# RMSNorm and matmul on one core: six of each sixteen tiles turned on VectorE in place of four

## The chip, the cores and the metric

The kernel runs on one core of one Trainium2 chip. The metric is device time in microseconds for one execution. Within a core, TensorE multiplies matrices, VectorE, ScalarE and GpSimd work element by element, and DMA engines move data between the chip's memory and the core; SyncE issues the DMA here.

## The reference

```python
# x: (16, 1024, 512) float32, weight: (512, 768) float32, gamma: (512,)
def reference(x, gamma, weight, eps):
    rms = np.sqrt(np.mean(x ** 2, axis=-1, keepdims=True) + eps)
    x_norm = x / rms * gamma
    return np.matmul(x_norm, weight).astype(np.float32)
```

There are 16,384 rows of 512 features. A tile is 128 rows, so there are 128 tiles. Gamma is multiplied into the weights once; the division by rms is done on the product, since it is one factor per row.

## The kernel before

Rows arrive in groups of sixteen tiles (`XG`) in two buffers. GpSimd casts a stretch to bf16. The matmul needs the features on the partitions, so each tile has to be turned. Two bf16 features are moved together as one 32-bit word, so a tile has two blocks of 128 by 128 words.

Most tiles are turned on TensorE: each word block is transposed into PSUM, between two matmuls of an earlier pair of tiles, and VectorE evicts the pair to SBUF. From the second group on, the last four tiles of each sixteen are turned on VectorE instead: GpSimd casts them to a buffer of their own, and VectorE moves them in sixteen steps, each of which transposes 32 by 32 blocks of all four tiles:

```python
    def quad_of(j):
        return j // 2 if (2 * j) % XG >= XG - 4 and 2 * j >= XG else None

    def cast_quad(q):
        quads[q] = quad_in.tile([P, 4, D], BF16, name="xq")
        nc.gpsimd.tensor_copy(out=quads[q], in_=held(x_tiles, XG, 4 * q, 4))
        turned = quad_out.tile([P, 4, 2, P, 2], BF16, name="xTq")
        # ... words and out_words: the same tiles seen as 32-bit words
        for tokens in range(0, P, B):            # B = 32
            for features in range(0, P, B):
                quad_moves.append((out_words[features:features + B, :, tokens:tokens + B],
                                   words[tokens:tokens + B, :, features:features + B]))

    def move_quad(n):
        for _ in range(min(n, len(quad_moves))):
            dst, src = quad_moves.pop(0)
            nc.vector.transpose(out=dst, in_=src)

    def matmul(i, k, acc, lo, hi):
        nc.tensor.matmul(out=acc[:, lo:hi], lhsT=xT_tiles[i // 2][:, i % 2, k // 2, :, k % 2],
                         rhs=w_bf[:, k, lo:hi], start=(k == 0), stop=(k == K - 1))
```

A tile takes eight matmuls (four feature blocks by 512 and 256 columns) into one of three accumulators in PSUM. ScalarE scales the even tiles by 1/rms and VectorE the odd ones, and the result is stored in stretches of eight tiles, shorter ones at the start and the end. The order of work is fixed by the program, engine by engine. The loop runs over pairs of tiles:

```python
        for j in range(1, NP):                                  # NP = 64 pairs
            load_until((2 * j + AHEAD + XG - 1) // XG * XG)     # AHEAD = 20
            if j in (1, 2):
                cast(4 * j + 4, nc.gpsimd, 4)
            elif j % 8 == 4 and j + 4 < NP:
                cast(2 * j + 8, nc.gpsimd, 8)
            elif j % 8 == 6 and j + 2 < NP:
                cast(2 * j + 12, nc.gpsimd, 4)
            if (2 * j + 2) % XG == 0 and 2 * j + 2 < NT:
                cast_quad((2 * j + 2 + XG - 4) // 4)
            elif 2 * j >= XG:
                move_quad(3)
            # ... squares of pair j + 4 on ScalarE, and every fourth pair root and reciprocal
            # ... pairs 1 to 3 left out here
            elif j + 2 < NP and quad_of(j + 2) is None:
                feed = feeder([j + 2], two)       # transposes and eviction of pair j + 2
            else:
                feed = None
            for i, engine in ((2 * j, nc.scalar), (2 * j + 1, nc.vector)):
                a = accumulator()
                matmuls(i, a, range(K), feed)
                finish_tile(i, a, engine)         # scaling, and the store behind a stretch
```

Of the kernel before, what the change touches and what calls it, by code (L numbers as in the profile page):

```python
# [12 lines left out]
F32 = mybir.dt.float32  # L13
BF16 = mybir.dt.bfloat16
# [4 lines left out]
def kernel(  # L19
# [8 lines left out]
    nc = tc.nc  # L28
    P = 128

    x = x.flatten_outer_dims()
    out = out.flatten_outer_dims()
    N, D = x.shape
    _, O = out.shape
    K = D // P
    NT = N // P
    NP = NT // 2
    XG, OG = 16, 8
# [30 lines left out]
    quad_in = ctx.enter_context(tc.tile_pool(name="quad_in", bufs=2))  # L69
    quad_out = ctx.enter_context(tc.tile_pool(name="quad_out", bufs=2))  # L70
# [4 lines left out]
    x_tiles, xb_tiles, tp_tiles, rstd_of, xT_tiles, o_tiles, norm_sums = {}, {}, {}, {}, {}, {}, {}  # L75

    def held(tiles, group, i, n=1):
        return tiles[i // group][:, i % group:i % group + n, :]
# [8 lines left out]
    def load_until(i):  # L87
        while starts and starts[0] < i:
            load(starts.pop(0))

    def cast(i, engine, n=1):
        if i // 8 not in xb_tiles:
            xb_tiles[i // 8] = xbp.tile([P, 8, D], BF16, name="xb")
        engine.tensor_copy(out=xb_tiles[i // 8][:, i % 8:i % 8 + n, :], in_=held(x_tiles, XG, i, n))  # L94
# [13 lines left out]
    def norms(i, n):  # L108
        ssq = stats.tile([P, 10], F32, name="ssq")
        for t in range(n):  # L110
            square(i + t, ssq[:, t:t + 1])
        root(i, n, ssq)
# [32 lines left out]
    def transpose_tile(i):  # L145
        for h in range(2):
            transpose_word(i // 2, i % 2, h)
        evac(i // 2, i % 2, 1)

    B = 32
    quads, quad_moves = {}, []

    def quad_of(j):
        return j // 2 if (2 * j) % XG >= XG - 4 and 2 * j >= XG else None

    def cast_quad(q):
        quads[q] = quad_in.tile([P, 4, D], BF16, name="xq")
        nc.gpsimd.tensor_copy(out=quads[q], in_=held(x_tiles, XG, 4 * q, 4))  # L160
        turned = quad_out.tile([P, 4, 2, P, 2], BF16, name="xTq")
        for n in range(2):
            xT_tiles[2 * q + n] = turned[:, 2 * n:2 * n + 2]
        words = quads.pop(q).rearrange("p t d -> p (t d)").bitcast(F32).rearrange("p (a w) -> p a w", w=P)
        out_words = turned.rearrange("p t h m c -> p (t h m c)").bitcast(F32).rearrange("p (a m) -> p a m", m=P)
        for tokens in range(0, P, B):
            for features in range(0, P, B):
# [8 lines that stand above are left out]
    def scale(engine, dst, src, r):  # L176
        if engine is nc.scalar:
            nc.scalar.mul(out=dst, in_=src, mul=r)  # L178
        else:
            nc.vector.tensor_single_scalar(out=dst, in_=src, scalar=r, op=mybir.AluOpType.mult)  # L180
# [3 lines left out]
    def accumulator():  # L184
        return opsum.tile([P, 2, WIDE], F32, name=f"ops{next(turns) % 3}").rearrange("p a b -> p (a b)")
# [16 lines left out]
    def matmuls(i, acc, ks, feed=None):  # L202
        for k in ks:
            matmul(i, k, acc, 0, WIDE)
            if feed:
                feed()
            matmul(i, k, acc, WIDE, O)

    def finish_tile(i, acc, engine):
        scale(engine, out_tile(i), acc[:, :O], rstd_of[i])  # L210
        store(i)


    def feeder(pairs, gaps, alone=False):
        queue = [(j, t, h) for j in pairs for t in range(2) for h in range(2)]
        calls = iter(gaps)

        def feed():
            for _ in range(next(calls)):
                j, t, h = queue.pop(0)  # L220
                transpose_word(j, t, h)
                if alone and h == 1:
                    evac(j, t, 1)
                elif (t, h) == (1, 1):
                    evac(j)
        return feed

    with tc.manual_schedule():
        g_row = singles.tile([2, P, 2], F32)
        nc.scalar.dma_start(out=g_row, in_=gamma.rearrange("(h w c) -> h w c", w=P, c=2))  # L230
        nc.scalar.preload_act_table(AF.Sqrt)  # L231
        wv = weight.rearrange("(h w c) o -> w h (c o)", w=P, c=2)
        w_f32 = singles.tile([P, K, O], F32)

        def load_weights(h):
            nc.sync.dma_start(out=w_f32[:, 2 * h:2 * h + 2, :].rearrange("p c o -> p (c o)"), in_=wv[:, h, :])  # L236

        load_until(2)
        load_weights(0)
        load_weights(1)  # L240
        load_until(2 * XG)


        warm = singles.tile([P, WIDE], BF16)
        nc.vector.memset(warm, 0.0)
        eps_sb = singles.tile([P, 1], F32)
        nc.vector.memset(eps_sb, float(eps))  # L247
        ident_f = singles.tile([P, P], F32)
        make_identity(nc, ident_f)
        spare = accumulator()  # L250

        def warm_up(n):
            for _ in range(n):
                nc.tensor.matmul(out=spare[:, :WIDE], lhsT=warm[:, :P], rhs=warm, start=True, stop=True)  # L254

        w_bf = singles.tile([P, K, O], BF16)

        def weights(k, engine, lo=0, hi=O):
            scale(engine, w_bf[:, k, lo:hi], w_f32[:, k, lo:hi], g_sb[:, k % 2, k // 2:k // 2 + 1])


        warm_up(6)
        gp = tpsum.tile([P, 2, 2], F32, name="tp")
        for c in range(2):
            nc.tensor.transpose(out=gp[:, c, :], in_=g_row[:, :, c], identity=ident_f[:2, :2])  # L265
        g_sb = singles.tile([P, 2, 2], F32)
        nc.vector.tensor_copy(out=g_sb, in_=gp)  # L267
        cast(0, nc.gpsimd)
        cast(1, nc.gpsimd)
        cast(2, nc.gpsimd, 2)  # L270
        norms(0, 2)
        warm_up(4)
        transpose_tile(0)
        transpose_tile(1)
        warm_up(2)
        weights(0, nc.vector, 0, WIDE)
        weights(0, nc.vector, WIDE, O)
        weights(1, nc.scalar)
        acc = [accumulator() for _ in range(2)]
        for i in range(2):  # L280
            matmuls(i, acc[i], [0, 1])
        weights(2, nc.vector)
        weights(3, nc.scalar)
        norms(2, 2)
        cast(4, nc.gpsimd, 2)
        matmuls(0, acc[0], [2, 3])
        finish_tile(0, acc[0], nc.scalar)
        matmuls(1, acc[1], [2, 3], feeder([1], [2, 2], alone=True))
        finish_tile(1, acc[1], nc.vector)
        cast(6, nc.gpsimd, 2)  # L290

        mid, one, two, both = ([0, 0, 1, 1, 0, 1, 1, 0], [1, 1, 0, 1, 1, 0, 0, 0], [1, 0, 1, 0, 1, 0, 1, 0],
                               [1, 1, 1, 1, 1, 1, 1, 1])
        for j in range(1, NP):
            load_until((2 * j + AHEAD + XG - 1) // XG * XG)
            if j in (1, 2):
                cast(4 * j + 4, nc.gpsimd, 4)
            elif j % 8 == 4 and j + 4 < NP:
                cast(2 * j + 8, nc.gpsimd, 8)
            elif j % 8 == 6 and j + 2 < NP:  # L300
                cast(2 * j + 12, nc.gpsimd, 4)
            if (2 * j + 2) % XG == 0 and 2 * j + 2 < NT:
                cast_quad((2 * j + 2 + XG - 4) // 4)
            elif 2 * j >= XG:
                move_quad(3)
            if j < 4:
                norms(2 * j + 2, 2)
            for pair in norm_turns.get(j, []):
                norms_of_group(pair)
            if j < 3:  # L310
                feed = feeder([j + 1], mid if j == 1 else one, alone=j == 1)
            elif j == 3:
                feed = feeder([4, 5], both)
            elif j + 2 < NP and quad_of(j + 2) is None:
                feed = feeder([j + 2], two)
            else:
                feed = None
# [3 lines that stand above are left out]
                finish_tile(i, a, engine)  # L321
# [35 lines left out]
```

## Time and profile before

| | before |
|---|---|
| time, median of 3 | 210.8 us (210.73 to 211.62) |
| span of the profiled execution | 208.1 us |
| granted TensorE clock, mean | 0.991 |
| VectorE busy | 149.6 us |
| ScalarE busy | 144.5 us |
| GpSimd busy | 59.9 us |
| read and written in the chip's memory | 35.13 MB and 50.33 MB |

The page of the profile gives busy time for each engine (PE is TensorE, PEld its weight loads, DVE is VectorE, ACT is ScalarE, POOL is GpSimd), then the span in 40 slices whose digits are busy tenths, then the chain of work that ended last, and then groups of instructions: line, engine, operation, output and input, shape, count, busy time, mean in ns, and idle time ahead of them. A line of a timeline has its start in us, its length in us, engine, line of the program and operation; in square brackets stands the idle time before it and what ended that. Matmuls overlap in TensorE's pipeline, so the length of one is more than what it adds. Lengths of GpSimd are rough.

### The profile page before, as it was taken

How to read it: one execution, taken by the hardware profiler on the slowest of the kernel's cores; microseconds unless marked ns; L12 is line 12 of the kernel's file. 1: busy time of each engine (PE TensorE's matmuls, PEld its weight loads, DVE VectorE, ACT ScalarE, POOL GpSimd, SP SyncE). 2: the span in 40 equal slices, each digit the busy share in tenths (PEclk: the TensorE clock that was granted, in tenths of full speed). 3: DMA queues.
4: the chain of work that ended last, by engine and by line, in shares of the span. 5: the costliest groups of instructions: out<-in, count | busy, mean ns of one | idle time of the engine just before them, and what ended most of it. 6: DMA issues, size and time to landing. Idle time of an engine off the chain costs nothing.

```text
span 208.1 us, 3335 instructions
## 1 busy us (share of the span) xinstructions
PE 195.1 (94%) x1238; PEld 129.9 (62%) x1238; DVE 149.6 (72%) x255; ACT 144.5 (69%) x343; POOL 59.9 (29%) x34
## 2 busy tenths in 40 slices
PE   7899999996999999999999999999999999999930
PEld 2466776663666666676667666776667666776610
DVE  0456647997379984999579984999579984999520
ACT  4698897753977877677867877677867877673310
POOL 3237652003900390065200670007500373000000
PEclk9999999999999999999999999999999999999996
DMA  6999999999999999999999999999999999994996
GB/s 252 419 438 441 331 396 435 459 449 390 437 439 438 405 439 409 408 403 431 428 411 436 441 430 430 420 431 439 430 438 408 424 444 435 424 439 203 453 413 267
DMA packets 5490, 85.65 MB, mean 412 GB/s; under 512 B 610, under 2 KB 612, under 8 KB 1380
## 3 DMA queue, kind: packets, MB, share of 16 engines
q1 hardware_dynamic: 5472, 85.46, 97.4%
q8 instruction: 9, 0.15, 0.3%
q14 instruction: 5, 0.04, 0.0%
q10 hardware_dynamic: 4, 0.00, 0.0%
HBM read 35.13 MB, written 50.33 MB: 411 GB/s over the span
## 4 chain that ended last, share of the span: by engine, by line
PE 71%; DMA 21%; SPq 2%; ACT 1%; POOL 1%; DVE 0%; issue 0%; ACTq 0%; POOLq 0%
PE ops L198 63%; DMA xt<-in_x_dram 21%; PE tp L135 8%; SPq L83 1%; POOL xb L94 1%; DVE ot L180 0%; ACT jk L98 0%; SPq L236 0%; ACT ot L178 0%; POOLq L94 0%; ACTq L178 0%; ACTq L98 0%
## 5 line engine op out<-in xcount | busy, mean ns | idle before, releaser
L198 PE MATMUL ops<-w_bf,xT 128*128 128x512 bf16 (+1 forms) x800 | 147.7, 326 | 2.6 <-ACT ot L178 2.0
L198 PEld LDWEIGHTS <-xT 128*128 128x128 bf16 x800 | 78.3, 98 | 48.4 <-issue 3.0
L178 ACT ACTIVATE ot<-ops,rstd 128x768 f32<-128x768 f32 x64 | 57.6, 899 | 45.3 <-PE ops L198 44.6
L98 ACT ACTIVATE jk<-xt 128x512 bf16<-128x512 f32 x128 | 78.8, 619 | 6.2 <-DMA xt<-in_x_dram 6.2
L94 POOL CAST xb<-xt 128x2048 bf16<-128x2048 f32 (+3 forms) x21 | 46.3, 2218 | 113.0 <-DMA xt<-in_x_dram 113.0
L180 DVE TENSOR_SCALAR ot<-ops,rstd 128x768 f32<-128x768 f32 x64 | 64.8, 1013 | 12.5 <-PE ops L198 12.0
L135 PE MATMUL tp<-ident_f,xb 128*128 128x128 f32 x200 | 54.2, 276 | 0.8 <-POOL xb L94 0.7
L142 DVE COPY xT<-tp 128x1024 bf16<-128x1024 bf16 (+1 forms) x53 | 34.5, 654 | 24.8 <-PE tp L135 24.1
L174 DVE STREAM_TRANSPOSE xTq<-xq 32x256 f32<-32x256 f32 x112 | 48.7, 435 | 1.9
L198 PE MATMUL ops<-w_bf,xTq 128*128 128x512 bf16 x224 | 42.8, 326 | 0.0
L135 PEld LDWEIGHTS tp<-ident_f,xb 128*128 128x128 f32 x200 | 28.5, 143 | 4.9 <-POOL xb L94 2.5
L198 PEld LDWEIGHTS <-xTq 128*128 128x128 bf16 x224 | 22.0, 98 | 12.3
L98 ACT ACTIVATION_READ_ACCUMULATOR jk<-xt 128x1 f32 x128 | 24.4, 191 | 0.0
L160 POOL CAST xq<-xt 128x2048 bf16<-128x2048 f32 x7 | 13.3, 1894 | 0.0
L104 DVE RECIPROCAL rstd<-rms 128x8 f32<-128x8 f32 (+3 forms) x20 | 3.9, 193 | 7.7 <-ACT rms L102 7.5
L102 ACT ACTIVATE rms<-ssq,eps_sb 128x8 f32<-128x8 f32 (+3 forms) x20 | 6.0, 299 | 0.6
L254 PE MATMUL ops<-warm 128*128 128x512 bf16 x12 | 5.2, 587 | 1.2 <-DVE eps_sb L247 1.2
L254 PEld LDWEIGHTS <-warm 128*128 128x128 bf16 x12 | 1.4, 128 | 2.9 <-issue 1.7
L178 ACT ACTIVATE w_bf<-w_f,g_sb 128x768 bf16<-128x768 f32 x2 | 1.9, 935 | 1.4 <-DMA w_f<-in_weight_dram 1.1
L267 DVE COPY g_sb<-tp 128x4 f32<-128x4 f32 x1 | 0.2, 161 | 3.2 <-PE tp L265 3.2
L231 ACT ACT_TABLE_LOAD x1 | 1.3, 1283 | 1.3 <-PEq L338 1.3
L180 DVE TENSOR_SCALAR w_bf<-w_f,g_sb 128x512 bf16<-128x512 f32 (+2 forms) x3 | 1.4, 481 | 0.1
(10 smaller groups left out, 1.9 us busy)
## 6 DMA issues: line engine op xcount, KB each, us to landing
out_dram<-ot SPq DMA_DIRECT2D x13, 3072.0 KB, 15.8
xt<-in_x_dram SPq DMA_DIRECT2D x11, 2048.0 KB, 18.5
xt<-in_x_dram SPq DMA_DIRECT2D x2, 4096.0 KB, 20.2
out_dram<-ot SPq DMA_DIRECT2D x5, 1536.0 KB, 9.9
w_f<-in_weight_dram SPq DMA_DIRECT2D x2, 768.0 KB, 5.6
out_dram<-ot SPq DMA_DIRECT2D x2, 768.0 KB, 16.5
xt<-in_x_dram SPq DMA_DIRECT2D x2, 512.0 KB, 5.3
xt<-in_x_dram SPq DMA_DIRECT2D x1, 1024.0 KB, 9.2
```

The source lines that it names most:

```text
L94: engine.tensor_copy(out=xb_tiles[i // 8][:, i % 8:i % 8 + n, :], in_=held(x_tiles, XG, i, n))
L98: nc.scalar.activation(out=jk, in_=held(x_tiles, XG, i)[:, 0, :], func=AF.Square, accum_out=ssq)
L102: nc.scalar.activation(out=rms[:, :n], in_=ssq[:, :n], func=AF.Sqrt, scale=1.0 / D, bias=eps_sb)
L104: nc.vector.reciprocal(out=rstd[:, :n], in_=rms[:, :n])
L135: nc.tensor.transpose(out=tp_tiles[j][:, t, h, :], in_=words[:, lo:lo + P], identity=ident_f)
L142: nc.vector.tensor_copy(out=dst[:, t:t + n, :], in_=src[:, t:t + n, :])
L160: nc.gpsimd.tensor_copy(out=quads[q], in_=held(x_tiles, XG, 4 * q, 4))
L174: nc.vector.transpose(out=dst, in_=src)
L178: nc.scalar.mul(out=dst, in_=src, mul=r)
L180: nc.vector.tensor_single_scalar(out=dst, in_=src, scalar=r, op=mybir.AluOpType.mult)
L198: nc.tensor.matmul(out=acc[:, lo:hi], lhsT=xT_tiles[i // 2][:, i % 2, k // 2, :, k % 2], rhs=w_bf[:, k, lo:hi], start=(k == 0), stop=(k == ...
L254: nc.tensor.matmul(out=spare[:, :WIDE], lhsT=warm[:, :P], rhs=warm, start=True, stop=True)
```

## The change

Six of each sixteen tiles, three pairs in place of two, are turned on VectorE. This is meant to take more transposes from TensorE. The six are cast as one piece, one pair earlier than the four were, and the blocks that VectorE moves span six tiles instead of four, so there are still sixteen of them in a group. The two tiles between the first eight and these six are cast after them. Tiles 32 to 39 are cast as four and four instead of eight at once.

```diff
-    def quad_of(j):
-        return j // 2 if (2 * j) % XG >= XG - 4 and 2 * j >= XG else None
-
-    def cast_quad(q):
-        quads[q] = quad_in.tile([P, 4, D], BF16, name="xq")
-        nc.gpsimd.tensor_copy(out=quads[q], in_=held(x_tiles, XG, 4 * q, 4))
-        turned = quad_out.tile([P, 4, 2, P, 2], BF16, name="xTq")
-        for n in range(2):
-            xT_tiles[2 * q + n] = turned[:, 2 * n:2 * n + 2]
+    B, TURNED = 32, 6
+
+    def turned_on_vector(j):
+        return (2 * j) % XG >= XG - TURNED and 2 * j >= XG
+
+    def cast_to_turn(group):
+        first = (group + 1) * XG - TURNED
+        straight = quad_in.tile([P, TURNED, D], BF16, name="xq")
+        nc.gpsimd.tensor_copy(out=straight, in_=held(x_tiles, XG, first, TURNED))
+        turned = quad_out.tile([P, TURNED, 2, P, 2], BF16, name="xTq")
+        for n in range(TURNED // 2):
+            xT_tiles[first // 2 + n] = turned[:, 2 * n:2 * n + 2]
 ... (words, out_words and the sixteen moves as before, over six tiles)
             if j in (1, 2):
                 cast(4 * j + 4, nc.gpsimd, 4)
+            elif j == 12:
+                for i in (32, 36):
+                    cast(i, nc.gpsimd, 4)
             elif j % 8 == 4 and j + 4 < NP:
                 cast(2 * j + 8, nc.gpsimd, 8)
             elif j % 8 == 6 and j + 2 < NP:
-                cast(2 * j + 12, nc.gpsimd, 4)
-            if (2 * j + 2) % XG == 0 and 2 * j + 2 < NT:
-                cast_quad((2 * j + 2 + XG - 4) // 4)
-            elif 2 * j >= XG:
+                cast_to_turn(j // 8 + 1)
+                cast(2 * j + 12, nc.gpsimd, 2)
+            else:
                 move_quad(3)
 ...
-            elif j + 2 < NP and quad_of(j + 2) is None:
+            elif j + 2 < NP and not turned_on_vector(j + 2):
                 feed = feeder([j + 2], two)
```

More of the change, by code (lines that the diff above doesn't have):

```diff
@@ L148, in transpose_tile @@
         evac(i // 2, i % 2, 1)
-    B = 32
-    quads, quad_moves = {}, []
-    def quad_of(j):
-        return j // 2 if (2 * j) % XG >= XG - 4 and 2 * j >= XG else None
-    def cast_quad(q):
-        quads[q] = quad_in.tile([P, 4, D], BF16, name="xq")
-        nc.gpsimd.tensor_copy(out=quads[q], in_=held(x_tiles, XG, 4 * q, 4))
-        turned = quad_out.tile([P, 4, 2, P, 2], BF16, name="xTq")
-        for n in range(2):
-            xT_tiles[2 * q + n] = turned[:, 2 * n:2 * n + 2]
-        words = quads.pop(q).rearrange("p t d -> p (t d)").bitcast(F32).rearrange("p (a w) -> p a w", w=P)
+    B, TURNED = 32, 6
+    quad_moves = []
+    def turned_on_vector(j):
[7 more added lines that the diff above has]
+            xT_tiles[first // 2 + n] = turned[:, 2 * n:2 * n + 2]
+        words = straight.rearrange("p t d -> p (t d)").bitcast(F32).rearrange("p (a w) -> p a w", w=P)
         out_words = turned.rearrange("p t h m c -> p (t h m c)").bitcast(F32).rearrange("p (a m) -> p a m", m=P)
```

## The prediction

> **What bounds the kernel now.** I read the page first (busy time, the 40 slices, the chain), then the waits, then the timeline of single engines around one group of sixteen tiles. A pair j below is tiles 2j and 2j+1, and a group is eight pairs.
>
> ```profile
> PE 195.1 (94%) x1238; PEld 129.9 (62%) x1238; DVE 149.6 (72%) x255; ACT 144.5 (69%) x343; POOL 59.9 (29%) x34
> DVE  0456647997379984999579984999579984999520
> DMA  6999999999999999999999999999999999994996
> PE 71%; DMA 21%; SPq 2%; ACT 1%; POOL 1%; DVE 0%; issue 0%; ACTq 0%; POOLq 0%
> L135 PE MATMUL tp<-ident_f,xb 128*128 128x128 f32 x200 | 54.2, 276 | 0.8 <-POOL xb L94 0.7
> L174 DVE STREAM_TRANSPOSE xTq<-xq 32x256 f32<-32x256 f32 x112 | 48.7, 435 | 1.9
> ```
>
> TensorE is the bound: its longest idle stretch after the start is one of 2.01 us at 50.4 us, where ScalarE stood behind the third group of x; from 52.4 to 199.7 us it has none. DMA engines are nearly as full, and VectorE, 72% on average, has three or four slices in a row at 9 in every group. The chain shows TensorE's own rhythm:
>
> ```profile
> 71.71 5.85 PE ops L198 x36
> 77.56 0.11 PE tp L135
> 77.67 0.65 PE ops L198 x4
> ...
> 95.13 5.85 PE ops L198 x36
> ```
>
> Four matmuls take 0.65 us, a transposed word 0.11 us on top. A pair with its four words of transposing takes 8 x 0.65 / 2 + 4 x 0.11 = 3.04 us, one without them 2.60; six of the first and two of the second are 23.4 us, which is the distance of the two long stretches (95.13 - 71.71 = 23.42). The mean of 276 ns per transpose is therefore no price: matmuls overlap, and 0.11 us is what a word costs.
>
> VectorE in the stretch that turns tiles, from its timeline:
>
> ```profile
> 89.09 0.69 DVE L142 COPY xT<-tp 128x1024 bf16<-128x1024 bf16 x1
> 89.82 1.02 DVE L180 TENSOR_SCALAR ot<-ops,rstd 128x768 f32<-128x768 f32 x1
> 90.86 1.33 DVE L174 STREAM_TRANSPOSE xTq<-xq 32x256 f32<-32x256 f32 x3
> ...
> 97.09 1.34 DVE L174 STREAM_TRANSPOSE xTq<-xq 32x256 f32<-32x256 f32 x3
> 98.44 1.02 DVE L180 TENSOR_SCALAR ot<-ops,rstd 128x768 f32<-128x768 f32 x1
> 99.47 0.44 DVE L174 STREAM_TRANSPOSE xTq<-xq 32x256 f32<-32x256 f32 x1
> 100.80 1.02 DVE L180 TENSOR_SCALAR ot<-ops,rstd 128x768 f32<-128x768 f32 x1 [0.89 <-PE ops L198]
> ```
>
> Start to start, an eviction costs 0.73 us, a scaling 1.04, three blocks 1.37: 3.14 us per pair against TensorE's 3.04. VectorE is full here and slips about 0.1 us per pair. The single block at 99.47 is the sixteenth. It runs in pair 29, and the first turned pair is 30, whose first matmul starts at 100.60: 0.7 us to spare.
>
> [...] at 50.2 us ScalarE's ready scaling stood behind two squares that waited 4.32 us for DMA. [...] in the 2.01 us stall nothing passed the blocked matmul. [...] No transpose of another size is in the trace, but the evictions have a slope that fits: 420 ns at 512 bf16, 684 at 1024, which is 264 ns for 256 words of 32 bits, 1.03 ns per word.
>
> **The change, part by part.**
>
> *Transposes removed.* In each of groups 1 to 7 one pair more (13, 21, ... 61) is turned on VectorE: 4 words x 0.11 = 0.43 us less on TensorE per group. In group 1 it is lost, because TensorE then stalls at 50 us for x whose load is issued at 29.96, before anything has changed. Six remain: **-2.6 us**. Seven evictions leave VectorE.
>
> *Blocks grow.* 112 blocks go from 256 to 384 words. My estimate is 435 + 128 x 1.03 = 567 ns each; three take 1.37 + 0.40 = 1.77 us.
>
> *Blocks move.* This is the step I hold decisive. Before, moving was under its own `if`, so every pair from 8 on, except the one that casts, called move_quad(3): pairs 8 to 12 ran fifteen and pair 13 the last. Now it is the `else` of the chain of casts. In a group, pairs 7, 8, 9, 10, 11 run three each; pair 12 takes a cast branch (12 by name, later ones by j % 8 == 4) and moves nothing. The sixteenth block runs at pair 13, 21, 29, ... which is the first turned pair itself. It is emitted after the scaling of tile 2j-1, and VectorE is in order. A turned tile's first weights take all 128 partitions and all 128 tokens, so they need all sixteen blocks. TensorE has to stand from the end of pair 12 until VectorE has scaled tile 25 and moved one block.
>
> The length of that stand: the scaling of a tile starts about 0.20 us after the next tile's first matmul could have issued (tile 60's matmul at 100.60, tile 59's scaling at 100.80), 1.03 us to the next VectorE start, 0.57 for the block, and 0.18 as an estimate for the signal and the exposed weight load (weights to matmul is 0.11 at 194.2): 1.98 us.
>
> *VectorE slips first.* A pair with all its work now costs VectorE 1.77 + 0.73 + 1.04 = 3.54 us against 3.04. Set zero at the end of the last tile of pair 6, where its scaling starts on time. Scalings of the odd tiles then start at 3.54, 7.08, 10.62 and (a reciprocal falls in pair 10, whose eviction is shorter after it: 0.68 in place of 0.73) 14.11, for tiles 15 to 21. Pair 11 has no eviction: moves end at 16.92, tile 23 is scaled by 17.96. There are three accumulators, so tile 24 needs tile 21's scaling, which ends at 15.15; TensorE would start tile 24 at 14.6. That is a stall of 0.6 us. Tile 25 then ends at 17.96, its scaling at 19.0, the block at 19.57, and tile 26 starts at 19.74 where it would have started at 17.2: **2.54 us per group**, the 1.98 included.
>
> *By group.* Group 1: 19.74 us after 31.49 is 51.2, so tile 26 issues until 52.5; tile 27 waits until 52.4 for ScalarE anyway. Loss 0.1 to 0.2. Groups 2 to 6: nothing of this lies beside another wait, since TensorE had none: 5 x 2.54 = **+12.7 us**. Group 7: no cast falls in pair 60, so the last block runs there, but behind the late scaling of tile 119. TensorE loses 0.6 + 0.85 us. The store behind tile 119 is late too, about 1.9 us, and from that store on DMA carries the end (6.3 MB between 192 and 206 us): **+1.9 us**.
>
> *Casts.* Six tiles cast ahead of two make pairs 12, 20, ... ready later: 1.89 + 0.85 = 2.75 us for six (slope of 1893 and 3600 ns) plus 1.04, instead of 1.89, after landing. They are read about 10 us later. The block cast must be ready one pair earlier, at 32.5 us in group 1; it ends at 28.55 + 2.75 = 31.3. Splitting the cast of tiles 32 to 39 removes a wait of 0.26 us in a stretch that already stood. I count none.
>
> *DMA.* Bytes and order are unchanged. First halves of the loads land 24.3 to 25.3 us apart (casts at 90.43, 115.74, 140.01, 164.82), slower than TensorE's 23.4, so loads were losing their lead. A TensorE at 23.0 + 2.5 = 25.5 us per group is slower than this, and loads stop being a threat.
>
> Sum: 0.2 + 12.7 + 1.9 - 2.6 = +12.2 us; I take +11.7, as a block a little shorter takes the slip away sixteenfold.
>
> **Rivals.** (a) What the change is for: the last block is hidden, TensorE saves 2.6 us and the end moves to about 208.2. It needs the sixteenth block a pair early; the branches say otherwise. (b) DMA covers all: near 211. A DMA share of 1.00 to 1.01 from 60 to 120 us speaks for it; against it, TensorE waits for no data after 52.4, and a loss on TensorE isn't hidden by full queues. (c) Only the stand of 1.98 us, no slip before it: 5 x 1.98 - 2.6 = +7.3, 218 us. That is so if the larger blocks cost 30 to 40 ns less than estimated. (d) Blocks scale with size, 650 ns: VectorE is 16 x 0.08 = 1.3 us later in each group, and the time is near 229 us.
>
> **Range and chances.** The centre is 210.8 + 11.7 = 222.5 us. (c) gives the lower edge, 218; a little over half of the way to (d) the upper, 226.5. All but (a) and (b) are over 2% slower, so 0.95 for slower, 0.04 within 2%, 0.01 faster.
>
> **What would show it.** Right: the waits get a new row of TensorE or its weight load on VectorE's xTq line, six times, about 2 us each, at pairs 13 to 53 and none as long at 61; blocks at about 567 ns; scalings of odd tiles starting up to 2 us late in pair 11; the distance of groups near 25.5 us. Wrong: blocks done before the pair begins, waits of TensorE on ScalarE or DMA in their place, or a block far from 567 ns.

## The result and the profile after

The changed kernel takes **219.95 us** (median of 6 runs, 219.76 to 220.54) against 210.75 us for the kernel before; the ratio is 1.0439, with a 95% interval of 1.0415 to 1.0463. It is slower by 9.2 us, within the range that the prediction gave and 2.6 us under its centre.

From the page of the changed kernel, the same rows as shown of before: TensorE, the slices of VectorE and DMA, the chain by engine, and the two groups that the change touches.

```profile
PE 194.5 (89%) x1210; PEld 125.6 (58%) x1210; DVE 159.6 (73%) x248; ACT 144.6 (66%) x343; POOL 60.0 (28%) x35
DVE  0474669994799929995699947998399956999330
DMA  6999999999999999999999999999999999680996
DVE 46%; PE 26%; DMA 15%; issue 4%; ACT 3%; SPq 1%; POOL 1%; DVEq 0%; ACTq 0%
L175 DVE STREAM_TRANSPOSE xTq<-xq 32x384 f32<-32x384 f32 x112 | 63.7, 569 | 1.9
L135 PE MATMUL tp<-ident_f,xb 128*128 128x128 f32 x172 | 46.7, 277 | 0.5 <-POOL xb L94 0.5
```

TensorE has 28 transposes less and a lower share. VectorE has 10 us more to do: 15.0 us more in blocks, which take 569 ns instead of 435, and 5.1 us less in evictions. It has taken TensorE's place on the chain. DMA, which had one slice at 4 before, now has slices at 6, 8 and 0 near the end.

The list of waits of the changed kernel shows what is new (who waited for whom: us in total, times, longest):

```profile
PEld L199 <- DVE xTq L175: 13.6, 7, 2.1
PE ops L199 <- DVE xTq L175: 10.9, 7, 1.7
PE ops L199 <- DVE ot L181: 1.5, 7, 0.2
```

None of the three stood in the list of before. The first two are one event seen by the weight load and by the matmul: seven times TensorE stands for a block. The third is an accumulator that VectorE frees late. Here is one group (pairs 28 to 30), TensorE first, then VectorE:

```profile
96.82 2.76 PE L199 MATMUL ops<-w_bf,xT 128*128 128x512 bf16 x16 [0.22 <-DVE ot L181]
101.28 2.99 PE L199 MATMUL ops<-w_bf,xTq 128*128 128x512 bf16 x17 [1.70 <-DVE xTq L175]
```

```profile
95.76 1.01 DVE L181 TENSOR_SCALAR ot<-ops,rstd 128x768 f32<-128x768 f32 x1
96.80 1.74 DVE L175 STREAM_TRANSPOSE xTq<-xq 32x384 f32<-32x384 f32 x3
98.57 2.07 DVE L181 TENSOR_SCALAR ot<-ops,rstd 128x768 f32<-128x768 f32 x2
100.65 0.57 DVE L175 STREAM_TRANSPOSE xTq<-xq 32x384 f32<-32x384 f32 x1
```

Pair 28 starts at 96.82, 0.22 us after the last matmul before it had ended, when VectorE's scaling that began at 95.76 is done. Pair 28 ends at 99.58. VectorE then scales its odd tile, and only behind this, at 100.65, moves the sixteenth block. Pair 29 starts at 101.28. In time lost, each idle stretch costs 0.165 us more than it shows, because a matmul that nothing holds started about that much before the recorded end of the one ahead (in the profile of before, pair 30's first at 100.60 us, the one ahead ending at 98.65 + 2.11 = 100.76): 0.385 and 1.87 us, 2.25 in a group. The next such restart is at 126.52, so a group takes 25.24 us; TensorE's work alone takes 23.0.

### The profile page after: what moved, and what is told of

It is laid out like the page before. It is cut to its first block, busy times and chain, and to the rows that moved or that the text cites. A ratio compares the mean times of both kernels' runs of the same rounds, so it can differ in the third digit from the quotient of the medians.

```text
span 217.6 us, 3270 instructions
## 1 busy us (share of the span) xinstructions
PE 194.5 (89%) x1210; PEld 125.6 (58%) x1210; DVE 159.6 (73%) x248; ACT 144.6 (66%) x343; POOL 60.0 (28%) x35
## 4 chain that ended last, share of the span: by engine, by line
DVE 46%; PE 26%; DMA 15%; issue 4%; ACT 3%; SPq 1%; POOL 1%; DVEq 0%; ACTq 0%
PE ops L199 24%; DVE xTq L175 21%; DVE ot L181 17%; DMA xt<-in_x_dram 15%; DVE xT L142 7%; ACT jk L98 2%; PE tp L135 2%; POOL xb L94 1%; ACT ot L179 1%; SPq L83 1%; DVE rstd L104 1%; SPq L237 0%; DVEq L181 0%; SPq L196 0%; ACTq L179 0%
## 5 line engine op out<-in xcount | busy, mean ns | idle before, releaser
L199 PE MATMUL ops<-w_bf,xT 128*128 128x512 bf16 (+1 forms) x688 | 127.4, 326 | 2.0 <-DVE ot L181 1.5
L199 PEld LDWEIGHTS <-xT 128*128 128x128 bf16 x688 | 67.3, 98 | 42.8 <-issue 3.6
L199 PE MATMUL ops<-w_bf,xTq 128*128 128x512 bf16 x336 | 61.2, 326 | 11.0 <-DVE xTq L175 10.9
L94 POOL CAST xb<-xt 128x1024 bf16<-128x1024 f32 (+3 forms) x22 | 40.6, 1855 | 103.7 <-DMA xt<-in_x_dram 103.7
L175 DVE STREAM_TRANSPOSE xTq<-xq 32x384 f32<-32x384 f32 x112 | 63.7, 569 | 1.9
L199 PEld LDWEIGHTS <-xTq 128*128 128x128 bf16 x336 | 32.3, 98 | 32.6 <-DVE xTq L175 13.6
L135 PE MATMUL tp<-ident_f,xb 128*128 128x128 f32 x172 | 46.7, 277 | 0.5 <-POOL xb L94 0.5
L142 DVE COPY xT<-tp 128x1024 bf16<-128x1024 bf16 (+1 forms) x46 | 29.4, 641 | 13.5 <-PE tp L135 13.0
L135 PEld LDWEIGHTS tp<-ident_f,xb 128*128 128x128 f32 x172 | 24.6, 144 | 4.1 <-POOL xb L94 2.0
L161 POOL CAST xq<-xt 128x3072 bf16<-128x3072 f32 x7 | 19.2, 2747 | 12.5 <-DMA xt<-in_x_dram 12.5
## 6 DMA issues: line engine op xcount, KB each, us to landing
out_dram<-ot SPq DMA_DIRECT2D x5, 1536.0 KB, 10.2
```

Source lines behind the costliest of these rows:

```text
L135: nc.tensor.transpose(out=tp_tiles[j][:, t, h, :], in_=words[:, lo:lo + P], identity=ident_f)
L142: nc.vector.tensor_copy(out=dst[:, t:t + n, :], in_=src[:, t:t + n, :])
L161: nc.gpsimd.tensor_copy(out=straight, in_=held(x_tiles, XG, first, TURNED))
```

## The experiments

All times are medians. The kernel before, measured beside each of them on the same chip, took 210.6 to 210.9 us, and each ratio is to that, with its 95% interval.

**1. The sixteenth block one pair earlier.** Moving gets its own condition again:

```diff
             elif j % 8 == 6 and j + 2 < NP:
                 cast_to_turn(j // 8 + 1)
                 cast(2 * j + 12, nc.gpsimd, 2)
-            else:
+            if j % 8 != 6:
                 move_quad(3)
```

> The changed kernel with moving under its own condition (every pair except those with j % 8 == 6), so that the sixteenth block runs in pair 12, 20, ... as it does in the last group of the changed kernel. Theory (the place of the block in VectorE's order makes TensorE stand): the stand of about 2 us behind one scaling goes; what stays is what the changed kernel shows in its last group, 0.21 us for an accumulator and about 0.7 to 1.0 us at the first turned pair, because VectorE is late. A group then takes 23.0 + 1.2 = 24.2 us on TensorE, and the time is near 215.3 us (214 to 216.5). Rival (VectorE simply has too much to do in a group, wherever the block stands): within 1 us of the changed kernel's 220. Rival (DMA sets the new pace): also near 220, with TensorE or ScalarE waiting for x.

Measured: 214.91 us (ratio 1.017, 1.013 to 1.021). The waits of this run and TensorE in the same group:

```profile
PE ops L199 <- DVE xTq L175: 4.7, 7, 0.7
PE ops L199 <- DVE ot L181: 1.6, 7, 0.2
```

```profile
95.89 2.76 PE L199 MATMUL ops<-w_bf,xT 128*128 128x512 bf16 x15 [0.22 <-DVE ot L181]
99.32 2.99 PE L199 MATMUL ops<-w_bf,xTq 128*128 128x512 bf16 x17 [0.67 <-DVE xTq L175]
```

The stand of 1.70 us became 0.67, a group takes 24.21 us, and 5.0 of the 9.2 us are back. What is left has another cause: the block now runs ahead of the scaling of the tile before it (98.69 against 99.29 us), and VectorE is simply not done yet. Runs 4 and 5 test this.

**2. The old kernel with its last block late.** Nothing is larger and nothing is saved; the leftover block alone moves into the first turned pair:

```diff
-            elif 2 * j >= XG:
+            elif 2 * j >= XG and j % 8 != 5:
                 move_quad(3)
```

> The kernel before, four tiles turned and small blocks, with its one leftover block put off from pair 13, 21, ... to pair 14, 22, ..., the first turned one. Nothing else differs: same instructions, same bytes. Theory: TensorE stands in all seven groups for 0.20 + 1.03 + 0.44 + 0.18 = 1.85 us, 13 us together, of which about 1 is hidden at the tail: 222 to 224 us. Rival (larger blocks and VectorE's load make the loss, not the place of the block): within 1 us of 210.8.

Measured: 220.94 us (ratio 1.0469, 1.043 to 1.0508), 10.2 us more and 1 us under the range expected. TensorE in this run:

```profile
105.23 0.39 PE L198 MATMUL ops<-w_bf,xTq 128*128 128x512 bf16 x1 [1.56 <-DVE xTq L174]
```

The place of a single block of 0.44 us costs as much as the whole change. The distance of these restarts, 80.07 to 105.23 us, is 25.16, so each costs 25.16 - 23.42 = 1.74 us and not 1.85: a weight load of 0.1 us that I had counted isn't exposed (the block ends at 104.73 + 0.44 = 105.17, the matmul starts at 105.23). VectorE kept program order there: the block stood behind a scaling for which VectorE waited 1.34 us, though the three blocks of the same tiles ahead of it had run at 99.99 us (scaling at 103.70, block at 104.73). In the first group the restart came at 54.91 where before it was 53.67, 1.24 us later, as TensorE had resumed 0.49 us earlier from its stall at 50 us. At the end 1.4 us are hidden: from VectorE's last scaling to the end of the span it is 7.0 us here (211.31 of 218.3) and 8.4 before.

**3. The split cast alone.** The kernel before with tiles 32 to 39 cast as four and four:

```diff
+            elif j == 12:
+                for i in (32, 36):
+                    cast(i, nc.gpsimd, 4)
             elif j % 8 == 4 and j + 4 < NP:
                 cast(2 * j + 8, nc.gpsimd, 8)
```

> The kernel before with only the cast of tiles 32 to 39 split in four and four. Expected by every theory: within 0.4 us of 210.8; the wait of 0.26 us of TensorE's weight load for GpSimd at 53.9 us goes. If it were worth more, the cast would have held up the third group.

Measured: 210.17 us (ratio 0.996, 0.9938 to 0.9983). It is a gain of half a microsecond, a little more than expected. In its profile TensorE resumes at 51.86 us instead of 52.37, but the x that it waited for also landed 0.5 us earlier in that run, before the cast in question began. TensorE's last matmul ends 0.60 us earlier than before (199.04 against 199.64), 0.51 of it there at the restart already, and the span is 208.0 against 208.1. So the profile leaves 0.1 us for the cast, and where the half microsecond of the medians comes from stays open.

**4 and 5. Taking work off VectorE.** As run 1, and one odd tile per group, then two, is scaled on ScalarE. Run 5 takes the pairs with j % 8 of 0 and 2, which are the first and third pair counted from 8, not the "second and sixth" of its text:

```diff
-            for i, engine in ((2 * j, nc.scalar), (2 * j + 1, nc.vector)):
+            for i, engine in ((2 * j, nc.scalar),                                 # run 4
+                              (2 * j + 1, nc.scalar if j > 8 and j % 8 == 2 else nc.vector)):
+            for i, engine in ((2 * j, nc.scalar),                                 # run 5
+                              (2 * j + 1, nc.scalar if j >= 8 and j % 8 in (0, 2) else nc.vector)):
```

> As the run with the block one pair ahead, and in each group from the second on the odd tile of the third pair (21, 37, ...) is scaled on ScalarE instead of VectorE. That takes 1.04 us from VectorE ahead of the sixteenth block. Theory: VectorE is no longer late, TensorE stands at most 0.1 us per group, a group takes 23.0 to 23.2 us, and the transposes saved show as 2 to 2.6 us: 208 to 209.5 us. Rival (DMA, whose first halves landed every 24.3 to 25.3 us before, then sets the pace): TensorE and ScalarE wait for x in the late groups and the time stays at 210 to 212. Rival (VectorE overloaded): 214 or more.

Measured: 210.78 us (ratio 0.9991, 0.9976 to 1.0006). The stands shrank, but a group takes 23.29 us, 0.1 more than expected and 0.3 above the 22.99 that TensorE's work needs, and the time did not fall under that of before. In the profile, another part of this is TensorE's clock. Windows of run 4 around its stall (length; busy time of TensorE, weight loads, VectorE, ScalarE and GpSimd; then granted clock, DMA share, GB/s):

```profile
50.00:52.00 2.00, 0.12 (x2) 0.00 (x0) 0.00 (x0) 2.00 (x5) 1.94 (x2) 1.00 1.11 473
52.00:54.00 2.00, 1.84 (x10) 1.11 (x10) 0.29 (x1) 2.00 (x6) 2.00 (x2) 0.86 1.00 430
54.00:56.00 2.00, 2.00 (x9) 1.15 (x8) 0.93 (x2) 1.65 (x6) 2.00 (x1) 0.50 1.03 442
```

Behind an idle stretch of 2.04 us the granted clock fell to 0.50 for 3.4 us. At 0.50 four matmuls and a transpose took 1.50 us (transposes at 53.89 and 55.39 us), at 1.00 they took 0.76 (56.87 and 57.63), so about half of the 3.4 us, some 1.7, is my estimate of the matmul time that it costs. TensorE ends at 200.22 us, 0.6 later than before.

> As the run with one scaling on ScalarE, but two odd tiles per group go there, those of the second and the sixth pair after the moving starts being counted from pair 8: j % 8 is 0 and 2 (tiles 17, 21, 33, 37, ...). In the run before this one TensorE still stood about 0.28 us per group for the sixteenth block, and in its profile the granted clock fell to 0.50 for some 3.5 us behind the idle stretch at 50 us. Theory: with 1.04 us more off VectorE the stand is gone, a group takes 23.0 us on TensorE in place of 23.29, and the time is 207.5 to 209.3 us (the clock's dip adds about 1 us when it comes). Rival (DMA sets the end once TensorE is faster): no stand of TensorE for VectorE, but ScalarE and TensorE wait for x in the last groups, and 210 to 211 us. Rival (ScalarE is overloaded, 2 x 0.90 us more per group): TensorE waits for ScalarE's scaling, 211 or more.

Measured: 210.79 us (ratio 0.998, 0.9952 to 1.0009). Here TensorE no longer waits for a block at all: the turned pairs begin at 73.69, 96.67, 119.66 us, 22.99 apart, which is the pace that the change was meant to give. TensorE ends 3 us earlier than before, at 196.64 instead of 199.64, and the time stands. The rival with DMA had this time right, but not its sign, as TensorE waits for no x behind 52.01 us. Windows of the kernel before at its end:

```profile
188.00:192.00 4.00, 4.00 (x27) 2.49 (x25) 3.85 (x8) 1.56 (x2) 0.00 (x0) 1.00 0.49 209
196.00:200.00 4.00, 3.64 (x23) 1.96 (x21) 1.34 (x2) 1.58 (x2) 0.00 (x0) 1.00 1.01 430
200.00:204.00 4.00, 0.00 (x0) 0.00 (x0) 0.70 (x1) 0.00 (x0) 0.00 (x0) 1.00 0.96 406
```

and of run 5:

```profile
188.00:192.00 4.00, 4.00 (x27) 2.43 (x26) 1.54 (x2) 1.38 (x2) 0.00 (x0) 1.00 1.02 436
196.00:200.00 4.00, 0.64 (x4) 0.20 (x2) 1.02 (x1) 0.28 (x1) 0.00 (x0) 1.00 1.00 424
200.00:204.00 4.00, 0.00 (x0) 0.00 (x0) 0.00 (x0) 0.00 (x0) 0.00 (x0) 0.61 0.80 338
204.00:205.00 1.00, 0.00 (x0) 0.00 (x0) 0.00 (x0) 0.00 (x0) 0.00 (x0) 0.50 0.20 86
```

Before, DMA is half idle from 188 to 192 us (share 0.49, 209 GB/s), waiting for TensorE to finish a stretch of tiles. In run 5 the pause is shorter and earlier (a share of 0.84 from 184 to 188 us, against 0.97 before); from 188 to 200 us DMA moves 418 to 436 GB/s, and from 203 us it runs out: the mean share of its 16 engines is 0.32, 0.20, 0.12 and 0.03 in the four microseconds that follow. So stores still lie in DMA's queues when TensorE has ended, and the last of them take a small part of what the engines can do. Why these lag isn't shown. The tail behind VectorE's last scaling began 8.4 us before the span's end in the kernel before (199.68 of 208.1), and 11.3 in run 5 (196.68 of 208.0).

**6. The changed kernel with VectorE on time.** The sixteenth block stays late, and one odd tile per group goes to ScalarE (the line of run 4, on the changed kernel).

> The changed kernel, the sixteenth block still in the first turned pair, with the odd tile of pairs 10, 18, 26, ... (j % 8 == 2) scaled on ScalarE, so that VectorE isn't late there. Theory (two terms in each group, an accumulator that VectorE frees late, 0.385 us, and the stand behind one scaling and one block, 1.87 us, which doesn't depend on VectorE's lateness): the first goes, the second stays in full; the last group loses about 0.9 us less; 5 x 0.385 + 0.9 = 2.8 us less than 219.95, so 217.1 (216.4 to 217.9). Rival (one cause, VectorE's load): both shrink, and the time is 215 or less.

Measured: 217.57 us (ratio 1.0314, 1.0271 to 1.0358). TensorE in the same group:

```profile
93.37 5.80 PE L199 MATMUL ops<-w_bf,xT 128*128 128x256 bf16 x35
100.87 2.99 PE L199 MATMUL ops<-w_bf,xTq 128*128 128x512 bf16 x17 [1.70 <-DVE xTq L175]
```

The accumulator's wait is gone (one unbroken stretch of 5.80 us), the stand is 1.70 us to the digit, and a group takes 24.86 us: 0.38 less. The time is 0.5 us above the centre expected and inside its range. These are two terms with two causes.

**7. Loads in halves.** As run 5, with groups 2 and 3 of x in halves (`for g in (1, 2, 3, 4, 5, 6, 7)` in the table of loads).

> As the run with two scalings on ScalarE, and the loads of the third and fourth group of x come in halves of eight tiles, as the later ones do, not in one piece of sixteen. Theory: x for tiles 32 to 39 lands some microseconds before 50 us, so the idle stretch of 2 us of TensorE at 50 to 52 us shrinks or goes, with the dip of the clock behind it: 1.5 to 3 us less than that run, 205 to 207.5 us. Rival (DMA is the bound by then): the 2 us come back as waits for x in later groups, the same time within 1 us.

Measured: 210.26 us (ratio 0.9959, 0.9938 to 0.998). The stall at 50 us is gone, and TensorE stands for ScalarE later instead:

```profile
142.28 1.68 PE L199 MATMUL ops<-w_bf,xTq 128*128 128x512 bf16 x9 [0.64 <-ACT ot L179]
167.19 1.68 PE L199 MATMUL ops<-w_bf,xTq 128*128 128x512 bf16 x9 [1.68 <-ACT ot L179]
```

ScalarE in turn waited for DMA, 7.3 us in all for x and 5.4 us for stores that had not yet left an output buffer, where run 5 had 6.1 and 2.1. The turned pair at 71.23 us was 2.46 ahead of run 5's; by 167 us this was handed back, and VectorE's last scaling starts at 196.97 us against 196.68. The rival of that run was right.

**8 and 9. Less for DMA to do.** Run 5 and the kernel before, each without the store of tiles 72 to 79. These rows of the output are not written; all else is computed.

```diff
-        if i == first + n - 1:
+        if i == first + n - 1 and i // OG != 9:
             nc.sync.dma_start(out=rows(out, first, n), in_=held(o_tiles, OG, first, n))
```

> The run with the block one pair ahead and two scalings on ScalarE, and the store of tiles 72 to 79 left out (3.1 MB of 85.5, so those rows of the output are not written). In that run TensorE took 22.99 us per group and ended at 196.6 us in place of 199.7, but the time stayed at 210.8: DMA engines were busy throughout and ran out one after another between 203 and 207 us. Theory (DMA sets the end there): without this store the backlog is gone, the tail behind TensorE's end is the 8.4 us of the kernel before again, and the time falls to about 207.7 us (207 to 208.7). Rival (the end is set by something behind TensorE that doesn't depend on bytes, or the granted clock): within 0.6 us of 210.8.

> The kernel before with the same store of tiles 72 to 79 left out. Theory (TensorE sets the end there; DMA had an idle stretch at 188 to 190.8 us): hardly any change, 209.8 to 210.9 us. Rival (DMA sets the end of the kernel before too): 2 us less or more.

Measured: run 5 falls from 210.79 to 208.07 us (ratio to the kernel before 0.9849, 0.9794 to 0.9904), the kernel before from 210.57 to 209.75 (0.9973, 0.9952 to 0.9993). With 3.1 MB less, 2.7 us appear in run 5, near the 3 us by which TensorE had ended earlier there. The profile of this run shows the tail short again:

```profile
188.00:192.00 4.00, 4.00 (x27) 2.43 (x26) 2.86 (x4) 0.90 (x1) 0.00 (x0) 1.00 0.47 197
198.64 1.02 DVE L181 TENSOR_SCALAR ot<-ops,rstd 128x768 f32<-128x768 f32 x1 [1.58 <-PE ops L199]
```

DMA is half idle again (0.47) and the last scaling starts 7.8 us before the end of the span (206.4), not 11.3. TensorE itself is later than in run 5, as this profile has a pause of 2.81 us at 50 us and a fall of the clock at its end. Of the four executions two, this one among them, took 208.95 and 208.68 us with a mean clock of 0.982, and two 207.46 and 207.20 with 0.992 and 0.990, so the 2.7 lies between two kinds. The old kernel, which TensorE bounds, gains 0.8, a little more than expected, and its DMA idles more in turn: a share of 0.23 from 188 to 192 us.

## Why the prediction was right, and where it was off

*The decisive step held.* The sixteenth block at the first turned pair makes TensorE stand behind one scaling and one block. It was put at 1.98 us, and measured at 1.87 (1.70 idle and 0.165). The 0.11 between them is the weight load that I took for exposed: the weights and the matmul of the restart both start at 101.28 us. Run 1 took it away and got 5 us back; run 2 made it in the old kernel with nothing else changed and lost 10 us.

*The slip of VectorE held in kind and was too big.* The term was 0.56 us per group (2.54 less 1.98) and measured 0.385; run 6 removed it alone. It is the difference of two times, and the prediction had both wrong. On VectorE I priced every pair at 3.54 us. The first took 3.28:

```profile
31.33 1.01 DVE L181 TENSOR_SCALAR ot<-ops,rstd 128x768 f32<-128x768 f32 x1
32.25 1.72 DVE L175 STREAM_TRANSPOSE xTq<-xq 32x384 f32<-32x384 f32 x3
34.00 0.69 DVE L142 COPY xT<-tp 128x1024 bf16<-128x1024 bf16 x1
34.61 1.01 DVE L181 TENSOR_SCALAR ot<-ops,rstd 128x768 f32<-128x768 f32 x1
```

The blocks began 0.92 us after the scaling's start and not 1.04, and the next scaling 0.61 after the eviction's and not 0.73. The third pair took 3.39 us (scalings at 38.14 and 41.53). So tile 21's scaling began at 13.69 on the prediction's clock (45.02 less 31.33), not 14.11, and its accumulator was free 0.4 us earlier than predicted. On TensorE, zero was set where pair 6's scaling "starts on time". It started 0.2 us late, behind the eviction of 30.72 us, so TensorE was ready for tile 24 at 14.4 (45.87 less 0.165 and 31.33), not 14.6. Together, 0.4 us less on one side and 0.2 on the other bring 0.56 down to 0.385.

*The sum.* For groups 2 to 6 the prediction had 12.7 us; measured are 5 x 2.25 = 11.25. Group 7 cost TensorE 1.22 us (0.385, and 0.67 + 0.165 at its turned pair) where I had 1.45, raised to 1.9 for a late store. But the tail behind the last scaling was 8.4 us in both profiles (209.20 of 217.6 after the change), so this raise was for nothing. Group 1 gained 0.26 us instead of losing 0.2: tile 28 started at 53.41 us, 0.22 ahead of the transpose at 53.63, and at 53.67 before. Whether the change has a part in this isn't shown: x had landed 0.25 us earlier in this profile (ScalarE's squares at 49.95 against 50.20), and in the profiles with this stall TensorE resumed anywhere between 51.86 and 52.64 us. With -2.6 for the transposes this makes 9.6 us; the two spans, 217.6 and 208.1, differ by 9.5. All the errors lie on one side, and the half microsecond that I took off the sum of 12.2 covered a fifth of them.

*Two readings.* The row of VectorE's slices has at most three digits of 9 in a row, not "three or four". And 6.3 MB is what the last three stores hold; from 192 to 206 us DMA moved 5.8 MB. No term changes by these.

*Blocks and casts.* The 567 ns were an estimate that carried the evictions' 1.03 ns per word over to blocks; 569 were measured, which is (569 - 435) / 128 = 1.05 ns per word. The cast of six ended at 31.31 us, in time for the first blocks at 32.25. So rival (d), blocks of 650 ns, is out, and with a slip of 0.385 us rival (c), no slip at all, too.

*What was wrong in the rivals.* Under (a) I wrote that a hidden block would let the end move to about 208.2 us, and (b) I set aside because a loss on TensorE isn't hidden by full queues. That held here for a loss (9.2 us longer, DMA at 394 GB/s over the span in place of 412); a gain was hidden by them. Run 5 has the block hidden and TensorE at 22.99 us per group, and takes 210.8. The 2.6 us are real on TensorE and lost to DMA, which had no idle time left for them but at its uneven end; runs 7 and 8 show it from both sides. With the blocks in the right place no run here was more than 0.4% faster than the kernel before (run 7), and run 3 reached that with four tiles turned, as before.

*The clock.* The loss of run 4 through the clock is seen in its profile alone. Its other executions have mean granted clocks between 0.977 and 0.989, but these means don't tell, since they count the tail as well: in run 5, whose clock falls only at 200.9 us, behind the last matmul, the mean is 0.983. So how much of the 210.8 us the clock explains in run 4 stays open.

## What to carry to other kernels

When a condition is merged into another's `else`, list for each turn of the loop what runs there: a leftover instruction of half a microsecond that slides into its consumer's own turn costs what stands ahead of it in its engine's queue as well: 1.74 us each time in run 2, for a block of 0.44. Where an engine keeps program order, as VectorE did in that run (the block at 104.73 us, behind a scaling at 103.70), price an instruction that moves by what stands in front of it, not by its length. And before taking work off a bound engine, look at whether the next one, here DMA, has idle time to give: the largest that it had behind the start was a stretch of share 0.49 over 4 us.

## What the hardware showed that I had not expected

A pause of TensorE of nearly the same length lowered its granted clock in one profile and not in another. In run 4 the clock fell to 0.50 from 53.44 to 56.85 us, with matmuls running, behind a pause of 2.04 us; in run 8 from 52.11 to 55.52 us, at the end of a pause of 2.81 us (nine matmuls behind it took 3.08 us, and 1.68 behind the pause of run 5). Behind 2.01 us in the profile of before and 2.41 us in run 9 it stayed at 1.00. The times of the clock's changes tell these apart. The trace of before has it at full speed for 197.97 us up to 204.39, that of the changed kernel for 204.80 us up to 211.71: 58 and 60 times 3.413 us. The falls of runs 4 and 8 lasted one such step each. Counted in these steps from the changes of each profile (204.3 us in run 9 and 202.3 in run 8 at the end), run 4's pause lies whole in the step that ends at 53.44 us, and 2.27 us of run 8's in the one that ends at 52.11. That of before is cut by an edge at 50.79 us into 0.43 and 1.58 us, that of run 9 by one at 50.70 us into 0.53 and 1.88. So in these four profiles the clock fell behind the steps with 2.04 and 2.27 us of idle TensorE, and not behind those with 1.58 and 1.88. That a step is what counts is my reading of four pauses; where between 1.88 and 2.04 us the clock starts to fall, or whether there is one such point, isn't shown.

VectorE's distance from one start to the next isn't fixed. Three blocks began 0.92 us after a scaling's start at 32.25 us and 1.04 us after it at 46.06, and a scaling 0.61 us after an eviction's at 34.61 and 0.72 at 38.14. The early ones start up to 0.09 us before the recorded end of the instruction ahead. It needs no wait: at 45.02 us a scaling began 0.09 us before the end of an eviction (44.47 + 0.64), and VectorE had not waited since 32.25. What decides it stays open. It is small, but in a stretch where the engine has 0.5 us too much in each pair it halved that excess in the first pair.
